# X of slice 1 loaded in four quarters over two hardware queues, one early store halved in place of four, and a fresh PSUM tile for each warm-up multiplication, in a one-core weight-gradient kernel

## The chip, the core and the metric

The kernel runs on one core of one Trainium2 chip. The metric is the device time of one execution in microseconds (us). The kernel before was run three times: 161.35 us is the median, 161.24 the lowest and 161.46 the highest. One further execution was profiled, and all rows below come from it.

## The reference

```python
def reference(input, grad_output):        # (16, 512, 1024) and (16, 512, 768), float32
    grad_weight = np.einsum('bmk,bmn->kn', input, grad_output)
    return grad_weight.astype(np.float32) # (1024, 768)
```

The two leading axes are summed over together, so this is one product: X transposed (1024 x 8192) times G (8192 x 768). Inputs and output are float32; the kernel multiplies in bfloat16 and sums in float32.

## The kernel before, in words

**Slices and blocks.** X and G are cut along the 8192 summed rows into 64 slices of 128 rows. K (1024) is cut into two halves of four rows of 128, and N (768) into two halves of 384. A block is named by a letter or figure and a number `q` from 0 to 3: A and B are the first half of K, C and D the second; A and C use the left half of N, B and D the right. One TensorE multiplication takes a 128x128 piece of X as weights and 384 columns of G.

**Two kinds of slices.** The string `LOADS` has 32 entries of two slices each. The first four (`s`, slices 0 to 7) are multiplied plainly: 16 multiplications a slice. The other 28 (`P`) are done by a scheme that forms sums and differences of quarters of X and G on VectorE (`sum_x`, `sum_g`) and then needs seven products in place of eight: 28 multiplications a pair. In all 128 + 784 = 912 multiplications, all issued at L331 in `multiply`.

**The order is written out by hand.** The string `PLAN` is a list of tokens, and the loop at the end of the function carries them out one after the other; tokens of one engine keep that order on the chip. `C0@2.1` multiplies one piece for block C0 into PSUM bank 2 (which it opens); `A0@R.1` does so in a resident bank; `r0` to `r4` are the entries of `ROUNDINGS`; `x2.10` and `g0.10` are stages of the sums of pair 10; `fB1@2` fills a bank from a sum kept in SBUF (L309); `cB1` and `vB1` close a bank by a copy on ScalarE (L356) or by VectorE (L371, L376, L378, L364 and L366); `pA3` and `qA0` add a shared sum on GpSimd (L388).

**The first microseconds.** The plan begins

```python
PLAN = (
    "C0@2.1 A0@R.1 r0 r1 r3 B1@1.1 r2 A2@R.1 r4 A1@R.1 vB1 A1.1 D3@4.2 A0.1 C0.1 D0@3.1 B2@0.1 cC0 B2.1 D0.1 "
...
```

Slices 0 and 1 arrive as float32. For slice 0, G comes in two halves on the SP queue (L128, L130) into `gf`, and X (1024 columns, 512 KB) in one transfer on the ScalarE queue (L129) into `xf[0]`. For slice 1, X comes in one transfer on the ScalarE queue (L131) into `xf[1]`. VectorE and ScalarE round them to bfloat16 at L202 (`round_by`): first those of slice 0 that stand ahead of the plan, then `r0` (right half of G of slice 0), `r1` and `r2` (X of slice 1, columns 512 to 768 and 0 to 256, on VectorE), `r3` and `r4` (columns 768 to 1024 and 256 to 512, on ScalarE). All other loads are issued by GpSimd (L153, L154, L158, L160), which converts to bfloat16 on the way.

Before the plan, TensorE carries out 17 warm-up multiplications on constants (`WARMUP`, L136): one bfloat16 one of 512 columns, two float32 ones of 512 columns and 14 bfloat16 ones of 128 columns. Their results are not used. Here all 17 write one PSUM tile named `bank7`, taken from the pool once.

PSUM tiles come from a pool with one buffer for each name (`bufs=1`): whoever takes a tile of a name again gets the same bank, and the first writer of the new tile waits until those who used the old one are done.

The first five multiplications of the plan (C0, A0, B1, A2, A1) use slice 0. The sixth, the token `A1.1`, is the first on slice 1: it needs columns 128 to 256 of X of slice 1, so the rounding `r2`.

**Stores.** `store` (L291) sends one block of 128 x 384 float32 (192 KB) from SBUF to the output, on the SP queue. The first `HALVED` calls cut it into two transfers of 96 KB. The last five stores of the plan follow the closings of C0, C1, B1, block 5 of number 2 (which stores D2), B2 and B0.

Of the kernel before, what the change touches and what calls it, by code (L numbers as in the profile page):

```python
# [9 lines left out]
P = 128  # L10
# [67 lines left out]
WARMUP = [("b", 512), ("f", 512), ("f", 512)] + 14 * [("b", 128)]  # L78
PAIRS_HELD = 11
SUMS_HELD = 8  # L80
MERGED = 2
HALVED = 4
ASIDES = 7
RESIDENT = 3
FOLDED = True
# [3 lines left out]
def kernel(  # L89
# [6 lines left out]
    nc = tc.nc  # L96
    bf16 = mybir.dt.bfloat16
    f32 = mybir.dt.float32
# [4 lines left out]
    NH = N // 2  # L103
# [4 lines left out]
    X = input.rearrange("b m k -> (b m) k")  # L108
# [7 lines left out]
    psum = ctx.enter_context(tc.tile_pool(name="psum", bufs=1, space=bass.MemoryType.PSUM))  # L116
# [9 lines left out]
    xf = [pairs.tile([P, K], f32, name=f"xf{s}", tag="xp") for s in range(2)]  # L126
# [1 line left out]
    nc.sync.dma_start(out=gf[:, LEFT], in_=G[0:P, LEFT])  # L128
    nc.scalar.dma_start(out=xf[0], in_=X[0:P, :])  # L129
    nc.sync.dma_start(out=gf[:, RIGHT], in_=G[0:P, RIGHT])  # L130
    nc.scalar.dma_start(out=xf[1], in_=X[P : 2 * P, :])  # L131

    wps = psum.tile([P, 512], f32, name="bank7")
    for dt, cols in WARMUP:
        dtype = f32 if dt == "f" else bf16
        nc.tensor.matmul(  # L136
            wps[:, 0:cols],
            nc.const_aps.tensor(1.0, (P, P), dtype),
            nc.const_aps.tensor(1.0, (P, cols), dtype),
            start=True,  # L140
            stop=True,
        )
# [103 lines left out]
    def sum_of(p, q):  # L246
        if p in SLOT:
            return macc[:, SLOT[p], q, :]
        row = q if p in "AB" else Q + q
        return acc[:, row, LEFT if p in "AC" else RIGHT]  # L250
# [7 lines left out]
    prepared = set()  # L258
    opened = {(p, q): [] for p in streams for q in range(Q)}
# [22 lines left out]
    def last(p, q):  # L282
        return done[p, q] == len(streams[p])

    def store(p, q, c0, c1, engine):
        row = q if p in "AB" else Q + q
        at = 0 if p in "AC" else NH
        cuts = [c0, (c0 + c1) // 2, c1] if stores[0] < HALVED else [c0, c1]
        stores[0] += 1
        for d0, d1 in zip(cuts, cuts[1:]):  # L290
            engine.dma_start(out=OUT[:, row, at + d0 : at + d1], in_=sum_of(p, q)[:, d0:d1])  # L291
# [49 lines left out]
    def close(engine, p, q, queue):  # L341
        parts, carried = opened[p, q].pop(0)
        final = last(p, q) and not opened[p, q] and p not in ("1D" if FOLDED else "1")
        dst = sum_of(p, q)
        away = engine == "c" and not carried
        if away:
            assert not last(p, q)
            asides[p, q].append(free_asides.pop(0))
            dst = aside[:, asides[p, q][-1], :]
        for tile_, at, c0, c1 in parts:  # L350
            b = tile_[:, at : at + c1 - c0]
            to = dst[:, c0:c1]
            if engine == "c":
                assert carried or away
                assert not final or p in "ABC"
                nc.scalar.copy(out=to, in_=b)  # L356
            elif engine == "k":
                assert carried and not final and last("D", q) and not opened["D", q]
                d = sum_of("D", q)[:, c0:c1]
                (nc.vector.tensor_add if p == "C" else nc.vector.tensor_sub)(out=to, in0=b, in1=d)  # L360
                folded.add((p, q))
            elif final and p == "5":
                assert carried and {("6", q), ("7", q)} <= closed
                nc.vector.tensor_sub(out=to, in0=b, in1=sum_of("6", q)[:, c0:c1])  # L364
                d = sum_of("D" if FOLDED else "6", q)[:, c0:c1]
                nc.vector.tensor_sub(out=d, in0=b, in1=sum_of("7", q)[:, c0:c1])  # L366
                if FOLDED:
                    store("D", q, c0, c1, queue)
            elif final and (p, q) not in prepared:
                assert carried and (SHARED[p], q) in closed and (p != "D" or ("5", q) in closed)  # L370
                nc.vector.tensor_add(out=to, in0=b, in1=sum_of(SHARED[p], q)[:, c0:c1])  # L371
                if p in "BCD" and len(parts) == 2:
                    store(p, q, c0, c1, nc.sync if c0 == 0 else nc.scalar)
            elif carried:
                assert (p, q) not in prepared
                nc.vector.tensor_copy(out=to, in_=b)  # L376
            else:
                nc.vector.tensor_add(out=to, in0=b, in1=to)  # L378
        if final and p in "ABCD" and engine == "v" and (len(parts) == 1 or p == "A"):
            store(p, q, 0, NH, queue)  # L380
        if last(p, q) and not opened[p, q] and not (engine == "c" and p in "ABC"):
            closed.add((p, q))
        spilled.add((p, q))

# [12 lines left out]
    for token in PLAN:  # L397
        op, rest = token[0], token[1:]
        if op in "xg":
            stage, u = rest.split(".")  # L400
            (sum_x if op == "x" else sum_g)(int(stage), int(u))
        elif op == "r":
            round_by(*ROUNDINGS[int(rest)])
        elif op == "f":
            block, banks = rest.split("@")
            fill(block[0], int(block[1]), [int(b) for b in banks.rstrip("s").split("+")], banks.endswith("s"))
        elif op in "cvk":
            close(op, rest[0], int(rest[1]), nc.scalar if rest[2:] == "a" else nc.sync)
        elif op in "pq":
            add_shared(rest[0], int(rest[1]), op == "p", nc.scalar if rest[2:] == "a" else nc.sync)  # L410
        else:
            block, n = token.split(".")
            block, _, where = block.partition("@")
            multiply(block[0], int(block[1]), where, int(n))
# [34 lines left out]
```

## Time and profile before

| | |
|---|---|
| median of three runs | 161.35 us (161.24 to 161.46) |
| the profiled execution's own time | 161.48 us |
| its span, first to last instruction | 159.7 us |
| around the span | 1.78 us |
| TensorE (PE) busy | 154.6 us, 97% |
| VectorE (DVE) busy | 136.1 us, 85% |
| ScalarE (ACT) busy | 104.4 us, 65% |
| GpSimd (POOL) busy | 42.6 us, 27% |
| loads and stores | 33.40 MB moved, 209 GB/s in the mean |

Times in the profile are counted from the start of the span. In a row of the timeline stand the start, the time from the first start to the last end, the engine (PE for multiplications, PEld for their weight loads, SPq and ACTq for DMAs issued there), the line, the operation, the number of merged instructions and, in brackets, the idle time before it with what ended that. The ends of multiplications are modelled: consecutive ones overlap, so a group's count and the next start tell more than an end. The chain of waits is followed back from the last instruction and printed in order of time.

### The profile page before, as it was taken

What the parts mean: (1) busy time and instruction counts of PE and PEld (TensorE: products, weight loads), DVE (VectorE), ACT (ScalarE), POOL (GpSimd) and SP (SyncE); (2) the same over time, 40 slices, a digit from 0 to 9 for tenths busy, and PEclk for the clock granted to TensorE, in tenths of its full rate; (3) what the DMA queues carried; (4) which work ended last, traced back from release to release, by engine and by line L of the source; (5) the groups of instructions that cost most, each with busy time, mean ns of one, the idle gap of its engine ahead of it and who ended that gap; (6) DMA issues with size and microseconds to landing.
All of it is one profiled execution on the core that took longest, in us unless ns stands there. A gap on an engine that the chain in (4) does not pass through costs nothing.

```text
span 159.7 us, 2734 instructions
## 1 busy us (share of the span) xinstructions
PE 154.6 (97%) x931; PEld 91.2 (57%) x931; DVE 136.1 (85%) x316; ACT 104.4 (65%) x243; POOL 42.6 (27%) x77
## 2 busy tenths in 40 slices
PE   8899999999999999999999999999999999999990
PEld 3456656556555565665656565656566565656560
DVE  0514169999999999999999999989999899999992
ACT  3445238999999999967867585563465472339930
POOL 7442222222212222221222221222222100006930
PEclk9999999999999999999999999999999999999999
DMA  5999999999999999999999999999999999940696
GB/s 171 297 212 211 214 216 212 213 213 212 213 213 211 214 212 213 214 211 214 213 214 212 214 213 214 212 211 213 213 211 219 208 214 213 213 81 0 196 353 239
DMA packets 12829, 33.40 MB, mean 209 GB/s; under 512 B 1424, under 2 KB 4624, under 8 KB 12816
## 3 DMA queue, kind: packets, MB, share of 16 engines
q0 software_dynamic: 9360, 28.64, 90.7%
q1 hardware_dynamic: 3168, 3.54, 6.6%
q10 hardware_dynamic: 288, 1.05, 1.7%
q8 instruction: 7, 0.11, 0.3%
q14 instruction: 6, 0.05, 0.1%
HBM read 58.72 MB, written 3.15 MB: 387 GB/s over the span
## 4 chain that ended last, share of the span: by engine, by line
PE 91%; DMA 4%; DVE 2%; issue 1%; ACT 0%; ACTq 0%; DVEq 0%
PE bank L331 91%; DMA xf<-in_input_dram 4%; DVE acc L371 1%; DVE macc L364 0%; DVE xp L202 0%; ACT macc L356 0%; ACTq L129 0%; DVE acc L378 0%; DVE acc L366 0%; DVEq L371 0%
## 5 line engine op out<-in xcount | busy, mean ns | idle before, releaser
L331 PE MATMUL bank<-gp,xp 128*128 128x384 bf16 x576 | 105.4, 326 | 0.7 <-DVE xp L202 0.6
L331 PEld LDWEIGHTS <-xp 128*128 128x128 bf16 x576 | 55.8, 98 | 39.1 <-DVE xp L202 1.0
L331 PE MATMUL bank<-ge,xe 128*128 128x384 bf16 x336 | 65.9, 326 | 0.0
L331 PEld LDWEIGHTS <-xe 128*128 128x128 bf16 x336 | 32.7, 98 | 22.3 <-DVE xe L184 0.6
L309 ACT COPY bank<-macc 128x384 f32<-128x384 f32 x69 | 32.6, 489 | 10.4 <-DVE macc L378 6.2
L356 ACT COPY macc<-bank 128x384 f32<-128x384 f32 x64 | 29.4, 484 | 10.4 <-PE bank L331 10.1
L378 DVE TENSOR_TENSOR macc<-bank,macc 128x384 f32<-128x384 f32 x56 | 30.5, 554 | 1.2 <-PE bank L331 0.9
L154 POOL DMA_DIRECT2D xp<-in_input_dram x30 | 15.9, 529 | 52.6 <-DMA xp<-in_input_dram 21.9
L309 ACT COPY bank<-acc 128x384 f32<-128x384 f32 x46 | 21.8, 485 | 11.5 <-DVE acc L378 8.9
L356 ACT COPY acc<-bank 128x384 f32<-128x384 f32 x44 | 20.7, 480 | 11.4 <-PE bank L331 11.1
L153 POOL DMA_DIRECT2D gp<-in_grad_output_dram x30 | 15.9, 531 | 38.4 <-PE bank L331 17.2
L378 DVE TENSOR_TENSOR acc<-bank,acc 128x384 f32<-128x384 f32 x42 | 22.8, 553 | 1.9 <-PE bank L331 1.9
L184 DVE TENSOR_TENSOR xe<-xp 128x1024 bf16<-128x1024 bf16 x28 | 19.3, 689 | 1.0 <-DMA xp<-in_input_dram 0.9
L194 DVE TENSOR_TENSOR ge<-gp 128x768 bf16<-128x768 bf16 x28 | 15.5, 552 | 0.2 <-DMA gp<-in_grad_output_dram 0.2
L376 DVE COPY acc<-bank 128x384 f32<-128x384 f32 x9 | 5.0, 555 | 8.9 <-PE bank L331 8.9
L186 DVE TENSOR_TENSOR xe<-xe,xp 128x512 bf16<-128x512 bf16 x28 | 11.8, 421 | 0.3
L188 DVE TENSOR_TENSOR xp<-xp,xe 128x512 bf16<-128x512 bf16 x28 | 11.5, 419 | 0.0
L196 DVE TENSOR_TENSOR ge<-gp,ge 128x384 bf16<-128x384 bf16 x28 | 9.9, 353 | 0.2
L198 DVE TENSOR_TENSOR gp<-ge,gp 128x384 bf16<-128x384 bf16 x28 | 9.8, 354 | 0.2
L388 POOL TENSOR_TENSOR acc<-acc,macc 128x384 f32<-128x384 f32 x7 | 6.8, 1003 | 0.5 <-ACT acc L356 0.5
L388 POOL TENSOR_TENSOR macc<-macc 128x384 f32<-128x384 f32 x1 | 1.0, 1042 | 18.0 <-DVE macc L378 18.0
L202 DVE CAST gp<-gf 128x192 bf16<-128x192 f32 (+1 forms) x2 | 0.6, 310 | 4.9 <-DMA gf<-in_grad_output_dram 4.9
(23 smaller groups left out, 41.2 us busy)
## 6 DMA issues: line engine op xcount, KB each, us to landing
xp<-in_input_dram POOLq DMA_DIRECT2D x30, 512.0 KB, 16.7
gp<-in_grad_output_dram POOLq DMA_DIRECT2D x30, 384.0 KB, 16.7
out_dram<-acc SPq DMA_DIRECT2D x12, 192.0 KB, 2.1
xf<-in_input_dram ACTq DMA_DIRECT2D x2, 512.0 KB, 4.9
out_dram<-acc SPq DMA_DIRECT2D x8, 96.0 KB, 1.7
gp<-in_grad_output_dram POOLq DMA_DIRECT2D x3, 192.0 KB, 6.4
xp<-in_input_dram POOLq DMA_DIRECT2D x2, 256.0 KB, 7.8
gf<-in_grad_output_dram SPq DMA_DIRECT2D x2, 192.0 KB, 4.1
```

Source lines behind the costliest of these rows:

```text
L153: nc.gpsimd.dma_start(out=gp, in_=G[rows, :].rearrange("(p m) n -> p m n", m=2))
L154: nc.gpsimd.dma_start(out=xp, in_=X[rows, :].rearrange("(p m) k -> p m k", m=2))
L184: nc.vector.tensor_sub(out=xe[:, 0:2, :], in0=x[:, 1::-1, :], in1=x[:, 3::-2, :])
L186: nc.vector.tensor_sub(out=xe[:, 2, :], in0=xe[:, 0, :], in1=x[:, 0, :])
L188: nc.vector.tensor_add(out=x[:, 1, :], in0=x[:, 2, :], in1=xe[:, 2, :])
L194: nc.vector.tensor_add(out=ge[:, 0:2, :], in0=g[:, 0:2, :], in1=g[:, 1::2, :])
L196: nc.vector.tensor_add(out=ge[:, 2, :], in0=g[:, 3, :], in1=ge[:, 0, :])
L198: nc.vector.tensor_add(out=g[:, 1, :], in0=ge[:, 2, :], in1=g[:, 2, :])
L309: nc.scalar.copy(out=tile_[:, at : at + c1 - c0], in_=src[:, c0:c1])
L331: nc.tensor.matmul(tile_[:, at : at + c1 - c0], stat, mov[:, c0:c1], start=fresh, stop=True, skip_group_check=True,)
L356: nc.scalar.copy(out=to, in_=b)
L378: nc.vector.tensor_add(out=to, in0=b, in1=to)
```

## The change

```diff
-HALVED = 4
+HALVED = 1
...
-    nc.scalar.dma_start(out=xf[1], in_=X[P : 2 * P, :])
-
-    wps = psum.tile([P, 512], f32, name="bank7")
-    for dt, cols in WARMUP:
+    for engine, b in ((nc.sync, 4), (nc.scalar, 6), (nc.sync, 0), (nc.scalar, 2)):
+        cols = slice(b * P, (b + 2) * P)
+        engine.dma_start(out=xf[1][:, cols], in_=X[P : 2 * P, cols])
+
+    for n, (dt, cols) in enumerate(WARMUP):
         dtype = f32 if dt == "f" else bf16
+        wps = psum.tile([P, 512], f32, name="bank4" if n == 0 else "bank7")
         nc.tensor.matmul(
```

X of slice 1 is now loaded by four transfers of 128 KB, each of 256 columns: columns 512 to 768 and then 0 to 256 on the SP queue, behind the two halves of G; columns 768 to 1024 and then 256 to 512 on the ScalarE queue, behind X of slice 0. Each rounding `r1` to `r4` waits for its own quarter.

The warm-up takes a tile from the pool in each turn of its loop: the first of name `bank4`, the other 16 of name `bank7`. In the built program the warm-up has the same 17 multiplications in the same order; from the third on, each now waits for TensorE's own semaphore, at the count that the multiplication just before it adds when it is done. In the program before none of the 17 waits for anything.

The first store alone is cut in two, so the program has 17 store transfers in place of 20.

The rest of the diff is in `close`: a branch for a final closing on ScalarE of a block that GpSimd has prepared. No token of this plan takes it. The plan's text is the same, and the orders of the instructions on VectorE, ScalarE and GpSimd are the same but for the new transfers and the semaphores that the quarters bring.

More of the change, by code (lines that the diff above doesn't have):

```diff
@@ L355, in close @@
                 assert not final or p in "ABC"
+                assert (p, q) not in prepared or (final and carried and len(parts) == 1)
                 nc.scalar.copy(out=to, in_=b)
@@ L380, in close @@
             store(p, q, 0, NH, queue)
-        if last(p, q) and not opened[p, q] and not (engine == "c" and p in "ABC"):
+        if final and engine == "c" and (p, q) in prepared:
+            store(p, q, 0, NH, queue)
+        if last(p, q) and not opened[p, q] and (engine != "c" or p not in "ABC" or (p, q) in prepared):
             closed.add((p, q))
```

## Prediction

> **What bounds the kernel now.** I read the chain of waits first, since it tells which engine sets the end.
>
> ```profile
> 0.74 0.41 ACTq L129
> 1.15 0.03 issue
> 1.18 5.94 DMA xf<-in_input_dram
> 7.12 0.02 issue
> 7.14 0.51 DVE xp L202 x2
> 7.65 0.05 issue
> 7.70 80.68 PE bank L331 x493
> ...
> 155.26 0.29 issue
> 155.55 0.55 DVE acc L371
> 156.10 0.02 issue
> 156.12 0.56 DVE acc L371
> ```
>
> From 7.70 us on TensorE carries the chain almost to the end. What stands ahead of 7.70 is the single transfer of X of slice 1 (1.18 to 7.12), two roundings on VectorE (`r1`, `r2`) and the multiplication `A1.1`. At the end stand two closings on VectorE. Next, the timeline of TensorE for the same stretch:
>
> ```profile
> 1.16 3.62 PE L136 MATMUL bank<-const-float32-1.0 128*128 128x512 f32 x4
> 4.57 1.50 PE L136 MATMUL bank<-const-bfloat16-1.0 128*128 128x128 bf16 x14
> 5.91 1.17 PE L331 MATMUL bank<-gp,xp 128*128 128x384 bf16 x5
> 7.70 20.16 PE L331 MATMUL bank<-gp,xp 128*128 128x384 bf16 x123 [0.62 <-DVE xp L202]
> ```
>
> The warm-up runs without a gap into the plan's first multiplication at 5.91; five of these are done by 7.08, and TensorE then idles 0.62 us. This is all that quarters of X could give. From 7.70 the spacing is 20.00 / 123 = 0.163 us. The last of the 907 multiplications from there starts at 155.75, 148.05 us later, where 906 spacings make 147.3: so only about 0.75 us of stalls are left in the rest of the run. The third view is the one line of the warm-up, minimum, median and maximum duration in ns:
>
> ```profile
> L136 PE MATMUL bank<-const-bfloat16-1.0 x15: 219/311/584, 0.8 to 5.9; 128*128 128x128 bf16 x14, 128*128 128x512 bf16 x1
> ...
> L136 PE MATMUL bank<-const-float32-1.0 x4: 1057/1057/1058, 1.2 to 3.7; 128*128 128x512 f32 x4
> ```
>
> One small warm-up lasts 311 ns, but its successor starts 107 ns after it: they overlap. Taken singly, the rows change at 5.7 us: before it 311 ns and 107 apart, after it 219 ns and 58 apart, and the weight load falls from 147 to 98 ns.
>
> **The warm-up, the largest term.** With a new tile each turn, every warm-up from the third on waits until its predecessor has signalled. Overlap is gone; the period becomes duration, plus signal, plus start. No multiplication of this trace waits for the one just before it, so I build the price from its parts: the last warm-up's semaphore goes up 233 ns after its start (row: 219, so 14 more), and the multiplication at 6.435 starts 42 ns after the VectorE signal (6.393) that released it. That makes 219 + 14 + 42 = 275 ns in the fast form and 311 + 14 + 42 = 367 in the slow one. Step by step:
> - The first float32 one is issued as now, in two passes at 1.16 and 2.01; the second ends at 2.01 + 1.06 = 3.07. The next waits for it: 3.07 + 0.06 = 3.13. Its weights (rows of 0.33) were loaded ahead and can't be now. Between 0 and 0.33; I take 0.03, the lag of the first multiplication (0.78) behind its load (0.75). Passes at 3.16 and 4.01, end 5.07, against 4.78 now.
> - The 14 small ones start at 5.12, 5.49 and 5.85 in the slow form, then eleven times 0.275 later: the last at 8.88.
> - The plan's first multiplication follows 0.06 later, at 8.94 in place of 5.91. Five at 0.163 make 0.81, so `A1.1` starts at 9.75 in place of 7.70: **+2.05 us**.
>
> Behind the waiting warm-ups stands all of TensorE's queue, and behind that the VectorE and ScalarE closings, which wait for its banks; the idle 0.62 us hide part of the delay, and this is already in the 2.05.
>
> **X in quarters.** The four pieces carry the same 512 KB, two of them behind G on SP's queue. Today X of slice 1 lands at 7.12 and is rounded by 7.65 on VectorE and 7.86 on ScalarE. With TensorE not there before 9.75, the pieces may land 2 us later than now before they cost anything, and an earlier landing buys nothing. The two further issues on each queue (0.37 to 0.46 us each) end near 2.5, ahead of the first rounding at 4.22, so ScalarE's roundings don't move. Cost 0; without the warm-up's cover, from -0.62 (all idle time gone) to some +0.3 (the smaller pieces later by a tenth of the 2.6 us between the landings of X of slices 0 and 1).
>
> **Stores.** Three issues fewer at 147.5 to 151, each 0.34 to 0.44 us on SP. The issue at 151.00 starts when GpSimd's add is done (150.99), so the queue is up to date there in both programs, and the last three start within 0.02 us of the VectorE closings they wait for, after 0.29, 0.07 and 0.15 us of free queue. Whole transfers land 1.9 to 2.3 us after issue, the halves 1.6 to 1.7, but all eight are over by 152.2, and the end is the last store at 156.70. Cost 0, within 0.1 either way. The branch in `close` is never taken.
>
> **What is given back.** A TensorE that is 2 us later meets its loads earlier. Of the 0.75 us of stalls I count those behind a load or the sums made of it:
>
> ```profile
> PEld L331 <- DMA xp<-in_input_dram: 1.0, 4, 0.3
> ...
> PEld L331 <- DVE xe L184: 0.6, 2, 0.4
> ```
>
> These are waits of weight loads, most of them hidden behind running multiplications; the gaps that they leave between multiplications (at 29.97, 30.51, 51.51 and 126.15) add up to 0.35 us. I take these as gone, between 0 and 0.75. VectorE, busy 27.8 of 28 us from 32 to 60, begins that stretch with a wait for a TensorE bank at 21.4, so it moves along; it gives nothing back. Loads run on at 213 GB/s to 142 us and only gain distance.
>
> Sum: 2.05 - 0.35 = **+1.70 us**. On the profiled execution 161.48 + 1.70 = 163.18; that run lies 0.13 over the median, so I predict **163.1 us**.
>
> **The rivals.**
> (1) *The slow form stays.* The rows get fast at 5.7, after 4.9 us of dense work. If multiplications that wait for each other don't count as dense, the 14 take 0.367 each (the last at 9.89) and the plan's begin slow, at 107/58 = 1.84 times 0.163 = 0.30, for as long again: in 4.9 us 16 in place of 30, or 2.3 us. Then +1.70 + 1.06 + 2.3 = +5.1, about 166.4; with the slow form ending between, 164.4 to 166.4. For it: one period in the fast form has 0.053 us of streaming in 0.275. Against it: the float32 ones are dense up to 5.1, so by 5.7 most of the stretch that made the rows fast is unchanged. [...] 10%.
> (2) *The wait is nearly free, and the quarters count.* If a warm-up can start before its predecessor's signal is through, the period stays near 0.107. TensorE reaches the plan at about 6 us and again waits for X. `r2` then waits for one quarter alone: at best the whole 0.62 us goes, at least the one rounding ahead of it (0.21). Time 160.9 to 161.3, **faster**. It decides at the period at which `A1.1` would start at 7.70: (7.70 - 0.81 - 0.06 - 5.12) / 13 = 0.13 us. For it: a wait that is already met costs nothing in the trace (rows at 6.60 carry one at the usual spacing). Against it: every consumer of a bank in the trace starts after the signal, never before. [...] 7%.
> (3) *The loads set the pace.* The DMA queues are over nine tenths busy to 142 us; if the delay were only distance that TensorE now wastes, all 0.75 us of stalls go and +1.3 stays: 162.7, inside my forecast's own range.
>
> **How the numbers follow.** Forecast 83%, rival 1 10%, rival 2 7%. Within the forecast: the switch at another time (all 14 small ones fast -0.2, and more if it falls into the float32 ones, -0.6; all slow +1.0), the weights +0.3, what is given back +0.35 or -0.4, 20 ns more or less for a period 15 times 0.02 = 0.3. Together about +0.9 to +2.9: **162.3 to 164.3**, which leaves out rivals 1 and 2 and little of the forecast. Within 0.2% (0.32 us) is about what a measurement can't tell from no change. Rival 2 is faster at 4% and the same at 3%; of the forecast 1% might shrink to the same. Slower 92%.
>
> **What would show it.** In the profile of the changed kernel, the 14 small warm-ups start 0.27 to 0.37 us apart; the first multiplication at what is now L331 starts near 8.9 us and is followed by no wait for X; the spacing after it is 0.163 at once. If it starts before 6.9 the warm-up term is wrong; if the spacing is 0.3, rival 1 holds; if a stall of over 0.3 us shows behind the load of X, the quarters cost. The end stays two closings and a store after the last multiplication.

## The result and the profile after

The changed kernel takes 165.34 us (median of 6 runs, 164.63 to 165.76), beside 161.31 us for the kernel before (6 runs, 161.24 to 161.54): 1.0246 times as long, 95% interval 1.0222 to 1.0270. It is slower, as forecast, but by 4.0 us where 1.7 were forecast, outside the stated range. The profiled execution took 165.62 us with a span of 163.9, so 4.14 us more than that of before.

The chain of waits in the changed kernel (start, duration, what):

```profile
0.78 2.31 PE bank L138 x3
3.08 0.04 issue
3.13 2.09 PE bank L138 x2
5.22 0.04 issue
5.26 0.28 PE bank L138
5.54 0.04 issue
5.58 0.28 PE bank L138
...
9.42 0.27 PE bank L138
9.69 148.19 PE bank L333 x898
...
160.16 0.02 issue
160.18 0.56 DVE acc L374
```

The chain no longer begins with a load. It begins with the warm-up, one multiplication after the other, each 0.28 us long and 0.04 behind the one before; the period is 0.320 us. The end has the shape that it had. The timeline of TensorE and of VectorE around the start of the plan (start, duration, engine and line, number merged):

```profile
5.26 4.42 PE L138 MATMUL bank<-const-bfloat16-1.0 128*128 128x128 bf16 x14
9.48 4.35 PE L333 MATMUL bank<-gp,xp 128*128 128x384 bf16 x13
```

```profile
8.58 0.34 DVE L204 CAST xp<-xf 128x256 bf16<-128x256 f32 x1 [1.90 <-DMA xf<-in_input_dram]
10.14 0.29 DVE L204 CAST xp<-xf 128x256 bf16<-128x256 f32 x1 [1.22 <-DMA xf<-in_input_dram]
```

Two things stand here that the forecast did not have. The first 13 multiplications of the plan are 0.320 us apart in place of 0.163: TensorE is still in the slow form, up to 13.64 us. (Slow form is the prediction's name for the stretch in which multiplications take about twice as long; in the run with fresh tiles alone, below, the granted clock reads 0.50 there.) And the quarters land late: the roundings `r1` and `r2` start at 8.58 and 10.14 us, where the single transfer let them start at 7.14 and 7.35. Two windows of the changed kernel show the end of the slow form (window, length, busy time and instructions of PE, PEld, DVE, ACT and POOL, granted clock, DMA share, GB/s):

```profile
10.30:13.70 3.40, 3.40 (x13) 1.53 (x11) 0.69 (x2) 0.78 (x2) 1.52 (x3) 1.00 1.14 216
13.70:17.00 3.30, 3.30 (x22) 2.00 (x21) 0.56 (x1) 1.02 (x4) 0.59 (x2) 1.00 1.05 209
```

13 multiplications in the one, 22 in the other. The granted clock reads 1.00 in both, because before the first recorded change of an execution, here at 13.68 us, the column has nothing to go by; the spacing tells it: 0.320 us before 13.64, 0.163 from 13.83 on. After a recorded fall, as with fresh tiles alone, it reads 0.50.

### The profile page after: what moved, and what is told of

It reads as the page before. It is cut to its first block, busy times and chain, and to the rows that moved or that the text cites. A ratio compares the mean times of both kernels' runs of the same rounds, so it can differ in the third digit from the quotient of the medians.

```text
span 163.9 us, 2737 instructions
## 1 busy us (share of the span) xinstructions
PE 158.5 (97%) x931; PEld 92.5 (56%) x931; DVE 136.0 (83%) x316; ACT 104.3 (64%) x243; POOL 42.5 (26%) x77
## 4 chain that ended last, share of the span: by engine, by line
PE 95%; DVE 1%; issue 1%; DVEq 0%
PE bank L333 90%; PE bank L138 5%; DVE acc L374 1%; DVE macc L367 0%; DVE acc L381 0%; DVE acc L369 0%; DVEq L374 0%
## 5 line engine op out<-in xcount | busy, mean ns | idle before, releaser
L333 PE MATMUL bank<-gp,xp 128*128 128x384 bf16 x576 | 106.9, 331 | 0.0
L333 PEld LDWEIGHTS <-xp 128*128 128x128 bf16 x576 | 56.9, 99 | 38.8 <-issue 2.5
L138 PE MATMUL bank<-const-bfloat16-1.0 128*128 128x128 bf16 (+1 forms) x15 | 4.3, 285 | 1.6 <-PEq L438 0.8
```

Source lines behind the costliest of these rows:

```text
L138: nc.tensor.matmul(wps[:, 0:cols], nc.const_aps.tensor(1.0, (P, P), dtype), nc.const_aps.tensor(1.0, (P, cols), dtype), start=True, stop=True,
L333: nc.tensor.matmul(tile_[:, at : at + c1 - c0], stat, mov[:, c0:c1], start=fresh, stop=True, skip_group_check=True,)
```

## The experiments

All times are medians beside runs of the kernel before on the same chip; ratios have a 95% interval.

**One warm-up tile.** This undoes the warm-up's part of the change and keeps the rest.

```diff
-    for n, (dt, cols) in enumerate(WARMUP):
+    wps = psum.tile([P, 512], f32, name="bank7")
+    for dt, cols in WARMUP:
...
-        wps = psum.tile([P, 512], f32, name="bank4" if n == 0 else "bank7")
```

> The changed kernel, but with one PSUM tile for all 17 warm-up multiplications as before: quarters of X and the single halved store stay. Theory 1, the fresh warm-up tiles are the whole cause: TensorE reaches the plan at 5.9 us, the quarters land no later than the single transfer did, and the time is that of the kernel before, 160.9 to 161.5 us. Theory 2, the quarters cost as much as their landing shows and were only covered by the slow warm-up: in the changed kernel the quarter for the rounding r2 landed at 10.12 us in place of 7.12, so A1.1 starts near 10.5 in place of 7.70, and with up to 0.75 us of later stalls given back the time is 163.3 to 164.1 us.

Its four runs took 163.63, 165.59, 166.50 and 166.60 us; before, 161.43. Theory 1 falls. The shortest is the profiled one, and its chain is that of theory 2:

```profile
2.11 7.78 DMA xf<-in_input_dram
9.89 0.02 issue
9.91 0.40 DVE xp L204
10.32 0.05 issue
10.36 145.52 PE bank L333 x893
```

TensorE reached the plan at 5.61, did five multiplications and stood until 10.36. That is 2.66 us later than 7.70 and gives 2.2 us at the end. The other three runs are 2 to 3 us longer still, which theory 2 had not foreseen. Their mean granted clock is 0.979 to 0.990, that of the shortest 1.000.

**Fresh tiles alone.** The kernel before with only the warm-up's part of the change (the same lines, the other way round).

> The kernel before, with a fresh PSUM tile for each warm-up multiplication alone: X of slice 1 stays one transfer, four stores are halved. Both theories: TensorE reaches the plan near 9.5 us, its first 13 or so multiplications are 0.32 us apart in place of 0.163, and the time is that of the changed kernel, 164.9 to 165.7 us. If it is under 164.8, the quarters cost something in the changed kernel too, through the loads behind them.

Measured: 165.01 us (163.97 to 165.88), 1.0245 times before, 1.0211 to 1.0278. This part alone costs about what the whole change costs. The profiled execution (163.97 us) has a recorded fall of the clock:

```profile
0.70:4.10 3.40, 3.26 (x4) 1.16 (x5) 0.00 (x0) 1.28 (x1) 2.86 (x6) 1.00 0.63 210
4.20:7.50 3.30, 2.70 (x12) 1.00 (x11) 1.76 (x7) 1.55 (x5) 1.43 (x3) 1.00 1.11 312
7.60:10.90 3.30, 3.13 (x12) 1.45 (x12) 0.56 (x1) 0.10 (x1) 1.64 (x4) 0.50 1.14 209
11.00:14.40 3.40, 3.40 (x22) 2.06 (x21) 0.56 (x1) 1.75 (x4) 1.33 (x3) 1.00 1.11 219
```

The clock rose at 4.13 us, so the small warm-ups ran 0.272 us apart; at 7.54, in the midst of them, it fell to a half, and at 10.95 it rose again. In between the plan ran 0.320 us apart. Two of the four runs have a mean granted clock of 0.986 and 0.987, which fits such a fall, and took 163.97 and 164.47 us. The other two read 0.999 and 1.000, as five of the six runs of the changed kernel do, and took 165.54 and 165.88. Busy time doesn't show this: PE is 2.70 of 3.30 us busy in the window ahead of the fall, because each small warm-up counts as busy for 0.23 us. What it streams is, by estimate, 54 ns in 272: 384 columns take 0.163 us in the dense part of the plan, so 128 would take a third of it.

**Longer serial warm-ups.** To tell the wait from the thin stream:

```diff
-WARMUP = [("b", 512), ("f", 512), ("f", 512)] + 14 * [("b", 128)]
+WARMUP = [("b", 512), ("f", 512), ("f", 512)] + 4 * [("b", 512)]
```

with fresh tiles as in the run above and the rest of the kernel before.

> The kernel before with a fresh PSUM tile for each warm-up multiplication, and the 14 small ones (128 columns each) replaced by 4 of 512 columns: each still waits for the one before it, but TensorE streams 0.21 of 0.43 us in the fast form (0.43 of 0.64 in the slow one) in place of 0.053 of 0.272. By count the warm-up ends near 7.0 to 7.5 us and A1.1 starts at 7.9 to 8.5. If the thin stream of the 14 is what made the slow form come back, it doesn't here: 161.4 to 162.3 us in all runs. If any wait of a multiplication for its predecessor does it, the slow form comes back and the time is 163.5 to 165 us.

Measured: 161.40 us (10 runs, 161.20 to 161.55), 1.0002 times before, 0.9992 to 1.0011.

```profile
5.26 1.88 PE L136 MATMUL bank<-const-bfloat16-1.0 128*128 128x512 bf16 x4
6.98 11.21 PE L331 MATMUL bank<-gp,xp 128*128 128x384 bf16 x68
```

Each warm-up still waits for the one before it (the last three start 0.43 us apart), the plan starts 1.1 us later than in the kernel before, and nothing is lost: the delay fits into the wait for X, and no slow form comes back. So it is not the wait by itself that costs, but 14 of them on short work. The two runs differ both in how thin the stream is and in how long the warm-up lasts (the plan starts at 6.98 and 8.53); the last section sets an estimate of the streaming beside the clock.

**Bridging the wait.** The run with one warm-up tile, with 54 small warm-ups in place of 14.

> The run with one warm-up tile (quarters stay, one halved store), with 54 small warm-up multiplications in place of 14, so that TensorE works on to about 8 us, nearer to the landing of the last quarter (9.9 us). If the slower runs of that kernel (165.6 to 166.6 us beside 163.63) are those in which TensorE fell back to the slow form while it waited 3.9 us for X, this kernel has none of them: all its runs lie at 163.3 to 164.0 us. If the spread came from the loads, it stays and the median is near 166.

Measured: 163.50 us (163.26 to 163.56), 1.0138 times before, 1.0122 to 1.0153. The spread is gone, all four granted clocks are 0.998 to 1.000, and all runs lie at the short end of the one above. So the long runs there are those in which TensorE fell to the slow form while it waited. The 2.2 us that are left are the price of the late X alone (`A1.1` starts at 9.99).

**Why X is late.** Four runs change the transfer of X of slice 1 alone, in the kernel before.

```diff
 (four quarters, all on the ScalarE queue)
+    for engine, b in ((nc.scalar, 4), (nc.scalar, 0), (nc.scalar, 6), (nc.scalar, 2)):
+        cols = slice(b * P, (b + 2) * P)
+        engine.dma_start(out=xf[1][:, cols], in_=X[P : 2 * P, cols])
 (four transfers of 32 partitions with whole rows)
+    for engine, r in ((nc.sync, 0), (nc.scalar, 1), (nc.sync, 2), (nc.scalar, 3)):
+        engine.dma_start(out=xf[1][r * 32 : (r + 1) * 32, :], in_=X[P + r * 32 : P + (r + 1) * 32, :])
 (two halves of the columns on two queues)
+    nc.scalar.dma_start(out=xf[1][:, 0 : 4 * P], in_=X[P : 2 * P, 0 : 4 * P])
+    nc.sync.dma_start(out=xf[1][:, 4 * P : 8 * P], in_=X[P : 2 * P, 4 * P : 8 * P])
 (one transfer in 1 KB pieces)
+    xq = accp.tile([P, 4, 264], f32, name="xq")
+    nc.scalar.dma_start(out=xq[:, :, 0 : 2 * P], in_=X[P : 2 * P, :].rearrange("p (b c) -> p b c", b=4))
```

> The kernel before with X of slice 1 in four quarters, all on the ScalarE queue behind X of slice 0, in the order columns 512, 0, 768, 256; one warm-up tile, four halved stores. If the small rows (1 KB in place of 4 KB a partition) are what made the quarters late, the last quarter lands 1 to 3 us after 7.12 here too, the quarter of r2 near 7 to 8.5 us, and the time is 161.3 to 162.5 us. If the queue is what made them late (two quarters waiting on SP behind G), the last lands near 7.1, that of r2 near 6, A1.1 starts at 7.1 to 7.4, and the time is 160.9 to 161.3.

> The kernel before with X of slice 1 in four transfers of 128 KB as in the changed kernel, the same two queues in turn, but each of 32 partitions with whole rows (4 KB) in place of 128 partitions with 1 KB. Each rounding now needs all four. Theory 1, a DMA engine takes one packet from each queue in turn, so small rows give a queue a small share: with 4 KB rows the last piece lands by 7.3 us, A1.1 starts by 7.9, and the time is 161.0 to 161.7 us. Theory 2, four transfers or the place behind G on SP are what is slow: the last piece lands at 8.5 to 10 us, as in the run with one warm-up tile (9.89), and the time is 162.5 us or more.

> The kernel before with X of slice 1 in two transfers of 2 KB rows: columns 0 to 512 on the ScalarE queue behind X of slice 0, columns 512 to 1024 on SP behind G. If each DMA engine takes one packet of each queue in turn (a 4 KB packet of the ScalarE queue lasts 0.16 us, one of GpSimd's queue 0.125, one of 1 KB 0.047), a round of two packets of 2 KB beside one of GpSimd's lasts about 0.3 us for 4 KB, as with whole rows: landings near 7.0 and 8.0, A1.1 at 8.0 to 8.6, time 161.6 to 162.6 us. If it is the number of transfers, they land as in the kernel before and the time is 161.0 to 161.4.

> The kernel before with X of slice 1 still in one transfer on the ScalarE queue, but written to a tile whose four pieces of 256 columns stand 264 apart, so that the transfer is made of 1 KB pieces in place of 4 KB; the roundings read that tile. Nothing else. Theory 1, the size of the pieces sets the queue's share: it lands at 9.5 to 11.5 us as the four quarters on this queue did (11.33), and the time is 163 to 166 us. Theory 2, the number of transfers is what costs: it lands near 7.1 and the time is that of before, 161.2 to 161.5.

| X of slice 1 | lands (last piece) | time, us | ratio to before |
|---|---|---|---|
| one transfer, 4 KB rows (before) | 7.12 | | |
| two halves, 2 KB rows, two queues | 8.40 | 164.44 (162.84 to 164.71) | 1.0174, 1.0133 to 1.0215 |
| four by partitions, 4 KB rows, two queues | 9.01 | 164.41 (162.84 to 164.52) | 1.0170, 1.0132 to 1.0209 |
| four quarters, 1 KB rows, two queues (one warm-up tile) | 9.89 | above | |
| one transfer, 1 KB pieces, one queue | 10.86 | 167.25 (166.94 to 167.65) | 1.0372, 1.0351 to 1.0392 |
| four quarters, 1 KB rows, one queue | 11.33 | 165.31 (164.81 to 166.45) | 1.0255, 1.0221 to 1.0289 |

The chain of the one transfer in 1 KB pieces:

```profile
1.19 9.67 DMA xq<-in_input_dram
10.86 0.02 issue
10.88 0.51 DVE xp L203 x2
11.39 0.05 issue
11.44 82.57 PE bank L332 x493
```

It has the same queue, the same bytes, one issue and one landing as the kernel before, and lands 3.74 us later. So small pieces alone make X late. The place behind G is not needed: the quarters on one queue, ahead of which only X of slice 0 stands, are 1.44 us later than those on two, though their last issue ends only 0.63 us later (3.17 and 2.54 us).

Small pieces are not the only thing that makes X late. The transfers by partitions have 4 KB rows and should have landed by 7.3; they landed at 9.01, where their theory 2 had them, so four transfers over the two queues cost 1.9 us even with whole rows. Their 4 KB packets took 0.23 to 0.30 us each in the mean between 5.5 and 6.5 us, where those of the single transfer took 0.17 to 0.18; why is not settled.

The landings carry this comparison, not the times. All runs of the last two rows of the table, and three of the four runs with halves and of the four by partitions, have a mean granted clock of 0.975 to 0.990, so a fall of the clock is in their times too; the runs without one, 162.84 us in both, are 1.5 us over the kernel before. All runs of these four rows took longer than the theory about sizes had forecast for them.

Counting the data packets that ended between 7.0 and 7.5 us in the traces (number, mean duration; GpSimd's are 1.5 KB, the others 1 KB):

```
                                GpSimd's queue    SP's queue       ScalarE's queue
changed kernel                  37, 0.134 us      41, 0.055 us     34, 0.046 us
one transfer in 1 KB pieces     48, 0.134 us      0                48, 0.059 us
four quarters on one queue      47, 0.145 us      0                54, 0.056 us
```

In these half microseconds a queue of 1 KB packets ended about as many packets as GpSimd's queue of 1.5 KB ones beside it: 34 and 41 beside 37, 48 beside 48, 54 beside 47. With smaller packets it moved less: the one transfer in 1 KB pieces moved 49 KB in that half microsecond, where the single transfer of the kernel before moved 131 KB between 5.5 and 6.0, in 32 packets beside 22.

**Without the neighbour.** The run with one warm-up tile, with GpSimd's loads held back by four copies of one column on GpSimd that wait for the four quarters.

> The changed kernel with one warm-up tile, and all loads of GpSimd held back until the four quarters of X of slice 1 have landed (four copies of one column on GpSimd ahead of them). The loads start some 6 us later, so the end is far later too (165 us or more) and says nothing; the landings do. Theory 1, GpSimd's packets take a turn between those of the quarters: without them the last quarter lands by 7.5 us in place of 9.9. Theory 2, small pieces are slow by themselves: the last lands at 9 us or later.

One execution, 166.21 us. The time from issue to landing of the four quarters, in the line of their source, is

```profile
DMA to landing us min/median/max: 4.7/4.7/4.9
```

where the changed kernel has

```profile
DMA to landing us min/median/max: 5.3/7.0/8.0
```

The last quarter lands at 6.83 us, in this one execution. So small pieces aren't slow by themselves; they are slow beside GpSimd's loads.

**The stores, alone.** `HALVED = 1` in the kernel before, and the same with three loads of one float on SP's queue.

> The kernel before with one early store halved in place of four, nothing else. Both theories: 161.2 to 161.5 us, no difference from before; the last store starts within 0.05 us after the last closing on VectorE. A rival, that whole stores fill the queue at the end, would show the last store landing later after its issue than 2.1 us, and 0.2 to 0.5 us more.

> The kernel before with one halved store, and three loads of one float each (never read) on SP's queue behind G, so that the program again has 24 transfers on the two hardware queues, as the kernel before (20 stores, 4 loads) and the changed one (17, 7); with one halved store alone it had 21. Theory 1, at the end SP waits for the eight transfer semaphores in a fixed order, and with 21 the last store is not the last that is waited for: three more waits of 0.06 us follow it. With 24 they come before it again: the time is 161.4 to 161.6 us, 0.15 to 0.25 under the run with one halved store alone (161.76). Theory 2, fewer halves make the landings late: the time stays at 161.7 to 161.8.

Measured: 161.76 us (9 runs, 161.43 to 161.98), 1.0021 times before, 1.0011 to 1.0030; with the three loads 161.51 us (12 runs, 161.19 to 161.74), 1.0002, 0.9993 to 1.0010. One halved store alone costs 0.3 us, which neither theory foresaw, and three useless loads bring it back. The trace shows where: at the end SP waits for the eight transfer semaphores in a fixed order, 0.06 us for each. With 24 transfers the last store's is the last; with 21, three more waits follow it (from 158.91 to 159.10). The last store's landing took 2.18 us after issue in place of 2.09, as the rival had it, but it takes as long with the three loads, whose time is that of the kernel before; so the landing is not what costs. The changed kernel has 17 stores and 7 loads, 24 again, so it doesn't pay the waits.

**Roundings swapped.** `r1` and `r2` change places in the plan of the kernel before, nothing else.

> The kernel before with one change in the plan: the tokens r1 and r2 change places, so that the rounding that the first multiplication on slice 1 needs is the first of the two after X of slice 1 lands. Nothing else. A1.1 starts 0.21 us earlier (7.49 in place of 7.70). If the start of TensorE sets the end one for one: 161.15 us against 161.35; if the stalls behind loads take it back, no difference.

Measured: 161.32 us (11 runs), 1.0000 times before, 0.9992 to 1.0009. `A1.1` starts earlier, but its own reason for waiting has changed:

```profile
7.53 4.75 PE L331 MATMUL bank<-gp,xp 128*128 128x384 bf16 x27 [0.62 <-DMA gp<-in_grad_output_dram]
```

It waits for G of slice 1, which GpSimd loads and which lands at 7.49 (7.47 in the kernel before). No version that I tried beats the kernel before.

## Why the prediction was wrong

**What held.** The sign, and the mechanism behind it: a fresh tile each turn takes away the overlap of the warm-ups (in the slow form they start 0.107 us apart before and 0.320 after). The start of the second float32 one was forecast at 3.13 to 3.16 and was 3.13. The period in the fast form was forecast at 0.275 and was 0.272 (fresh tiles alone). In the slow form it was 0.320, not 0.367: the 311 ns that I built it from are those of rows that overlap their neighbours; alone, such a multiplication lasts 264. What is given back came to 0.57 us (the 14th multiplication of the plan is 4.63 us later than before, the last one 4.06), within the stated 0 to 0.75, where I took 0.35. The end added 0.08, within the stated 0.1, but that was luck: the prediction did not look at the waits for the transfers, and they cost nothing only because the number of transfers is 24 again.

**The step that failed first** is the one that reads "the 14 small ones start at 5.12, 5.49 and 5.85 in the slow form, then eleven times 0.275 later". It took the change to the fast form at 5.7 us over from the kernel before, as if it were a time of day. It is not fixed: in the eleven traces whose warm-up uses one tile, and so begins in the same way, it came between 3.55 and 6.24 us. With fresh tiles in the same warm-up it came at 4.13 us in one execution, and at 13.68 in that of the changed kernel. In the profiled execution of the changed kernel all 14 ran in the slow form, and 13 multiplications of the plan after them, for which the prediction had the fast spacing at once:

| | forecast | measured |
|---|---|---|
| first multiplication of the plan | 8.94 | 9.48 |
| `A1.1` (7.70 before) | 9.75, +2.05 | 11.08, +3.38 |
| eight more in the slow form | 0 | +1.25 |
| given back | -0.35 | -0.57 |
| end | 0 | +0.08 |
| sum | +1.70 | +4.14 |

This was rival 1, which I gave 10%. Its own working was near: spacing 0.30 (0.320 measured), a stretch of 4.9 us (4.2), a time of 164.4 to 166.4. (Its term of 1.06 should be 1.01, 9.89 less 8.88.) The argument against it, that the float32 warm-ups are dense up to 5.1 us, was wrong: in the profiled execution of the changed kernel no rise is recorded before 13.68 us, and with fresh tiles alone, where one is at 4.13 us, the clock had fallen again, at 7.54, before the plan began at 8.53.

**The step that failed unseen** is "cost 0; without the warm-up's cover, from -0.62 to some +0.3" for X in quarters. The quarters cost 3.0 us of landing, ten times the bound, and 2.2 us of time where nothing covers them. I had priced the smaller pieces by bytes and issues, and not by the packets of GpSimd's loads that stand between them, though the profile's part on the queues lists them. Had the warm-up been as fast as I forecast, `A1.1` would have waited for X until about 10.48 (the rounding at 10.14, its 0.29 us and the lag of 0.05), not started at 9.75.

**The two hide each other.** Quarters without the slow form cost 2.2 us, fresh tiles alone 3.6 (165.01 beside 161.43), both together 4.0. Each delays the first multiplication on slice 1, the quarters to 10.36 us and the fresh tiles to 10.13 (11.08 in the changed kernel), and the later one counts. So undoing one of them brings little back: with one warm-up tile the kernel is slower than the changed one's median in three of four runs.

**Rival 2** was priced too high even had its condition held: behind X of slice 1 stands G of slice 1 at 7.47, so no earlier X could have won more than 0.2 us of the 0.62, and the swapped roundings show that not even this reaches the time.

Not tried: what makes the packets of the transfers by partitions slow. The long runs with two halves (164.4 to 164.7 beside 162.84) read a granted clock of 0.988 to 0.990 beside 0.999, which fits a fall of the clock, but only the shortest was profiled.

## What to carry to other kernels

A transfer that is waited for should go in large rows, and here in one piece: beside another queue's loads, cutting its rows in four made it land 3 to 4 us later, and four transfers of whole rows over two queues 1.9 us later, with the bytes unchanged. A scratch PSUM tile that is taken anew in each turn of a loop is a wait of each turn for the one before; here, with some 54 ns of streaming (an estimate) in each 272, the clock fell to a half in the midst of such turns, at 7.54 us with fresh tiles alone, and TensorE's busy time, 2.70 of 3.30 us, didn't show it. And before a part is priced at nothing because another covers it, price it without the cover: two faults of 2 to 4 us here hid behind each other.

## What the runs showed of the hardware

With fresh tiles alone, changes of the granted clock are recorded at 4.13, 7.54 and 10.95 us, 3.41 us from each other. In the kernel before the first recorded rise is at 5.71 us, in the changed kernel at 13.68.

For four stretches of that length that end at a change I worked out, from the starts of the multiplications, the share in which TensorE streams columns. These shares are estimates: for 128 columns I count the spacing of dense rows, 107 ns in the slow form and 54, a third of 0.163 us, in the fast one.

```
stretch, us (kernel)                           streaming    clock at its end
7.54 to 10.95 (fresh tiles alone)              80%          rises
2.35 to 5.76 (longer serial warm-ups)          78%          rises
5.41 to 8.82 (one transfer in 1 KB pieces)     34%          falls
4.13 to 7.54 (fresh tiles alone)               29%          falls
```

So the clock rose after the two fuller stretches and fell after the two thinner ones, in one execution of each kernel. A wait for X did not always bring a fall: in the transfer in 1 KB pieces, where TensorE idled 4.68 us ahead of 11.44, the granted clock reads 0.50 from 8.90 to 15.60; in the shortest run with one warm-up tile, where it idled 3.54 us ahead of 10.36, it reads 1.00 throughout, with 21 multiplications from 10.30 to 13.70.

What sets the time of a change is not shown: the changed kernel and the one with fresh tiles alone have the same warm-up, and the first rise is at 13.68 us in the one and at 4.13 in the other. Nor is it shown why runs of one program spread here, by 1.1 us in the changed kernel and by 3.0 with one warm-up tile.
